# A hybrid encoder layer: the out-projection by Strassen's seven products

## The chip, the cores and the metric

One core of a Trainium2 chip runs the whole kernel. The metric is the device time of one execution in microseconds (us): the median of three runs, and for where the time goes one profiled execution. TensorE is PE in the profile, VectorE DVE, ScalarE ACT, GpSimd POOL, and SP is the engine whose queue issues the transfers.

## The reference

One layer of a hybrid encoder: the input is projected (`w_in`), half of the heads are gMLP heads, half a state space model (SSD); their outputs side by side go through the out-projection `w_out` (2048 to 1024). Then come a residual sum with LayerNorm, a feed-forward part with a squared relu, and a residual sum with LayerNorm again.

```python
def layer_norm(x, g, b):
    ...
    y = (xf - mu) * lax.rsqrt(var + LN_EPS) * g.astype(jnp.float32) + b.astype(jnp.float32)
    ...
    out = jnp.einsum('ble,ed->bld', jnp.concatenate([y_g, y_s], axis=-1), w_out)
...
def squared_relu_ffn(x, w1, w2):
    h = jnp.square(jax.nn.relu(jnp.einsum('bld,df->blf', x, w1)))
    return jnp.einsum('blf,fd->bld', h, w2)
```

There are 2048 prompt tokens and 8 x 16 tokens of running streams, so 17 tiles of 128 tokens (`NCH`); `KD` is 8, a width of 1024 in tiles of 128. The scale of the SSD half's normalisation (`ssd_norm_g`) is multiplied into the rows of `w_out` that it meets.

## The kernel before

Every product in full precision is made of three matmuls (`PASSES`) of two parts: `split` (lines 55 and 56) rounds an operand on ACT into a first part and takes the rest on DVE as a second.

**Mixer** (`mixer_heads`). The tokens go in three blocks of 6, 6 and 5 tiles. In each block 18 weight units (x, z, u, v) are multiplied in a fixed order, and between units `run` takes one task of a list: an SSD step of a tile (`ssd`) or a gMLP step (`gmlp`). Block 0 splits the weights and stores the two parts (`keep_parts`); blocks 1 and 2 load the parts (line 117), which have twice the bytes of the raw weights. gMLP writes its outputs to DRAM by features (`yg`, 128 features x 128 tokens), SSD by tokens (`ys`). The last block's five gMLP tasks are left over as the tail.

**Out-projection** (`out_proj`). All of `w_out` is split once into eight tiles in SBUF (`load_w`, eight `wout` tiles). Token tiles go by groups, the first two and the last two together, the others one by one: `load_yg` and `load_ys` load a tile (SSD's by four transfers and a transposition by DVE, `flip`, line 43) and split it (`mx`); 96 matmuls of 128x512 (line 683) make its row of outputs; then come the residual sum and LayerNorm on DVE with scale and bias (`layer_norm`), and the store. The tail's tasks run within the first group. Beside it, `during_out_proj` makes in each group a piece of what FFN1 needs: four sums of a group of `w_ff1` weights (`w1_piece`, lines 777 to 780, on DVE, stored as `w1s`) and, three times, the sums of the transposed LayerNorm outputs (`x_piece`, stored as `xv`).

**FFN** (`ffn`). FFN1 is by Strassen's seven products already: for each of three token blocks and 16 weight groups, seven products of 12 matmuls (line 858), whose operands are the sums above. `load_x` and `load_w1` load and split them.

Order: each engine takes its instructions in one fixed order, which a scheduler has made from the order of the code and its own costs. SP issues all transfers in one such order; by the semaphores of the built program each transfer waits for the one eight before it.

## Time and profile before

| | us |
|---|---|
| median of three runs | 2825.11 (2823.72 to 2827.59) |
| the profiled execution | 2822.72 |
| its span | 2821.0 |
| PE busy | 2753.9 |
| DVE, ACT, POOL busy | 1816.1, 1096.0, 395.1 |
| mean granted clock of PE | 0.991 |

The 40 slices of the page show where PE is less than fully busy: the 8s at slices 16 and 21 are the beginning and the end of the out-projection, the last is the kernel's end.

```text
PE   9999999999999998999989999999999999999998
DVE  6766667645585457665558667667775356644887
ACT  5445423323333333100115556556665323333343
```

A digit is the busy share of a slice of 70.5 us in tenths; 9 is 90% or more. In a row of the groups of instructions the numbers behind the count are busy time and the mean of one in ns, then the idle time of the engine just before them and what ended it.

### The profile page before, as it was taken

How to read it: one execution, taken by the hardware profiler on the slowest of the kernel's cores; microseconds unless marked ns; L12 is line 12 of the kernel's file. 1: busy time of each engine (PE TensorE's matmuls, PEld its weight loads, DVE VectorE, ACT ScalarE, POOL GpSimd, SP SyncE). 2: the span in 40 equal slices, each digit the busy share in tenths (PEclk: the TensorE clock that was granted, in tenths of full speed). 3: DMA queues.
4: the chain of work that ended last, by engine and by line, in shares of the span. 5: the costliest groups of instructions: out<-in, count | busy, mean ns of one | idle time of the engine just before them, and what ended most of it. 6: DMA issues, size and time to landing. Idle time of an engine off the chain costs nothing.

```text
span 2821.0 us, 42133 instructions
## 1 busy us (share of the span) xinstructions
PE 2753.9 (98%) x15814; PEld 2525.6 (90%) x15814; DVE 1816.1 (64%) x2836; ACT 1096.0 (39%) x2024; POOL 395.1 (14%) x547
## 2 busy tenths in 40 slices
PE   9999999999999998999989999999999999999998
PEld 8988899999999997887879999999999888888886
DVE  6766667645585457665558667667775356644887
ACT  5445423323333333100115556556665323333343
POOL 2214223323233312000100000000000000000022
PEclk9999999999999999999999999999999999999999
DMA  9897888766697768888579858667877468855764
GB/s 316 257 297 250 281 288 272 228 221 217 218 305 220 244 218 302 279 260 273 159 217 342 292 214 286 222 223 259 276 233 259 152 233 300 299 173 190 272 206 171
DMA packets 492316, 699.83 MB, mean 248 GB/s; under 512 B 74560, under 2 KB 379088, under 8 KB 485584
## 3 DMA queue, kind: packets, MB, share of 16 engines
q1 hardware_dynamic: 492112, 697.14, 74.8%
q8 instruction: 124, 2.03, 0.3%
q14 instruction: 80, 0.66, 0.1%
HBM read 474.04 MB, written 223.00 MB: 247 GB/s over the span
## 4 chain that ended last, share of the span: by engine, by line
PE 77%; DMA 12%; DVE 6%; issue 1%; ACT 1%; POOL 1%; SPq 1%; DVEq 0%; ACTq 0%; POOLq 0%
PE pf L858 22%; PE pf L1075 22%; PE psfl L231 13%; PE pstl L239 10%; PE po L683 4%; PE yd L446 2%; DMA w1p<-in_w_ff 2%; DMA w1s<-w1p 2%; PE pf L1040 2%; DMA v<-v 1%; DMA xv<-xtt 1%; PE st L483 1%; DMA v<-vo 1%; DMA e<-at 1%; PE yo L489 1%
## 5 line engine op out<-in xcount | busy, mean ns | idle before, releaser
L858 PE MATMUL pf<-xt,w 128*128 128x384 f32 (+1 forms) x4032 | 671.8, 329 | 14.6 <-ACT w L55 11.4
L858 PEld LDWEIGHTS pf<-xt,w 128*128 128x128 f32 x4032 | 669.2, 189 | 17.4 <-ACT w L55 12.3
L1075 PE MATMUL pf<-w,ht 128*128 128x512 f32 x2688 | 618.2, 389 | 0.0
L1075 PEld LDWEIGHTS pf<-w,ht 128*128 128x128 f32 x2688 | 504.6, 188 | 104.6
L231 PE MATMUL psfl<-xw,w 128*128 128x384 f32 (+1 forms) x2880 | 494.9, 330 | 0.0
L231 PEld LDWEIGHTS psfl<-xw,w 128*128 128x128 f32 x2880 | 475.5, 188 | 9.0 <-issue 8.6
L239 PE MATMUL pstl<-w,xw 128*128 128x256 f32 (+1 forms) x3264 | 411.0, 286 | 8.4 <-ACT w L55 6.5
L239 PEld LDWEIGHTS pstl<-w,xw 128*128 128x128 f32 x3264 | 396.4, 190 | 21.0 <-issue 11.8
L683 PE MATMUL po<-wout,mx 128*128 128x512 f32 x1632 | 379.5, 394 | 12.0 <-ACT mx L55 8.1
L683 PEld LDWEIGHTS po<-wout,mx 128*128 128x128 f32 x1632 | 309.2, 190 | 79.1 <-ACT mx L55 8.8
L56 DVE TENSOR_TENSOR ht<-hr,ht 128x1536 fp32r<-128x1536 f32 (+1 forms) x84 | 132.3, 1577 | 128.0 <-ACT ht L55 126.5
L76 POOL TENSOR_SCALAR frs<-fmv 128x1 f32<-128x1 f32 x17 | 8.9, 524 | 1291.6 <-DVE fmv L996 1291.0
L55 ACT CAST ht<-hr 128x1536 fp32r<-128x1536 f32 (+1 forms) x84 | 112.2, 1337 | 194.7 <-PE pf L1075 142.0
L56 DVE TENSOR_TENSOR w<-w1s,w 128x512 fp32r<-128x512 f32 x192 | 132.0, 691 | 41.0 <-ACT w L55 36.0
L55 ACT CAST w<-w1s 128x512 fp32r<-128x512 f32 x192 | 118.3, 619 | 64.1 <-PE pf L858 57.0
L308 DVE SCALAR_TENSOR_TENSOR acc<-raw,cw,acc 128x640 f32<-128x640 f32 (+1 forms) x108 | 111.4, 1031 | 14.1 <-ACT acc L302 12.7
L56 DVE TENSOR_TENSOR w<-w2r,w 128x512 fp32r<-128x512 f32 x144 | 93.8, 686 | 36.8 <-ACT w L55 36.6
L55 ACT CAST w<-w2r 128x512 fp32r<-128x512 f32 x144 | 83.3, 618 | 87.3 <-PE pf L1075 56.9
L438 ACT ACTIVATE e<-e,nacum 128x128 f32<-128x128 f32 x272 | 83.6, 389 | 66.8 <-POOL e L69 66.7
L55 ACT CAST w<-w1r 128x512 fp32r<-128x512 f32 x96 | 59.4, 618 | 98.6 <-PE pf L858 95.3
L247 ACT ACTIVATE gt<-gt 128x256 f32<-128x256 f32 (+1 forms) x116 | 52.3, 451 | 95.9 <-DVE gt L246 95.9
L849 ACT ACTIVATE hc<-hc 128x384 f32<-128x384 f32 (+3 forms) x144 | 87.1, 608 | 1.8
(214 smaller groups left out, 2875.4 us busy)
## 6 DMA issues: line engine op xcount, KB each, us to landing
w1s<-w1s SPq DMA_DIRECT2D x48, 1024.0 KB, 6.7
hr<-hv SPq DMA_DIRECT2D x56, 768.0 KB, 6.1
w2r<-in_w_ff SPq DMA_DIRECT2D x112, 256.0 KB, 5.6
w<-w_x SPq DMA_DIRECT2D x12, 2048.0 KB, 10.5
w1r<-in_w_ff SPq DMA_DIRECT2D x48, 512.0 KB, 6.7
hv<-hs SPq DMA_DIRECT2D x32, 768.0 KB, 5.2
ws<-in_w_in SPq DMA_DIRECT2D x34, 512.0 KB, 7.7
e<-at SPq DMA_DIRECT2D x34, 512.0 KB, 6.7
```

What stands on the lines that cost most here:

```text
L55: nc.scalar.copy(hi, src)
L56: nc.vector.tensor_sub(lo, src, hi.bitcast(F32))
L231: nc.tensor.matmul(ps[:, :n], w[:, a, k, f * P:(f + 1) * P], xw[:, b, k, o:o + n], start=(q, i, k) == KORDER[0], stop=(q, i, k) == KORDER[-1])
L239: nc.tensor.matmul(ps[:, :n], xw[:, a, k, j * P:(j + 1) * P], w[:, b, k, :n], start=(q, i, k) == KORDER[0], stop=(q, i, k) == KORDER[-1])
L308: nc.vector.scalar_tensor_tensor(aa, raw[:, k:k + npr], cw[:, ft, k:k + 1], aa, op0=ALU.mult, op1=ALU.add)
L438: nc.scalar.activation(e[:, h], e[:, h], AF.Exp, bias=s["nacum"][:, i:i + 1])
L446: nc.tensor.matmul(yd[:, h * HD:(h + 1) * HD], e[:, h], xdt[:, h * HD:(h + 1) * HD], start=True, stop=True)
L683: nc.tensor.matmul(acc[c][d], m[c][k // 4][:, a, k % 4], W[q][:, w, i, d * 512:(d + 1) * 512], start=k == 0 and (a, w) == (0, 0), stop=k = ...
L849: nc.scalar.activation(t, t, AF.Square)
L858: nc.tensor.matmul(o, W[i][:, u, k], X[i][:, v, k, :n], start=q + k == 0 and not more, stop=q == 2 and k == 3, skip_group_check=True)
L1040: nc.tensor.matmul(ps[d], h[:, u, k, f], w[d][:, v], start=k + f + q == 0, stop=(k, f, q) == (n - 1, 1, 2))
L1075: nc.tensor.matmul(acc[l], h[:, u, m, j * P:(j + 1) * P], w[m][:, v], start=kg + q + m == 0, stop=(kg, q, m) == (3, 2, 3))
```

## The change

**Out-projection.** Tiles are taken in eight pairs: (0,3), (1,4), (2,5), (6,9), (7,10), (8,11), (12,14), (13,15); tile 16 is alone (`ODD`). A pair's rows, the two halves of the 2048 inputs (here: each half holds four feature tiles of gMLP and four of SSD) and the two halves of the outputs make a 2 x 2 product of matrices, which seven products of 24 matmuls (128x512) give. `seq` is their order: product 1, then 2, of the first six pairs; 1 and then 2 of the last two pairs and the odd tile; 0 of the odd tile; then 6, 7 and 5 of all pairs; then 4 and 3 by turns, and 3 of the odd tile. "(6,2)" is product 6 of pair 2. Each product has its own weight operand of eight tiles (`wo`), of which two sets fit; it is made from raw parts (`wor`, four buffers), for 6 with two subtractions whose results are stored (`wot`) for 5 and 4. The results are summed up in tiles `y` in SBUF (`evict`), by ACT for product 1 and DVE else.

**Sums of the left operand** (`mix`) are made in the mixer as tasks: for each pair four sums of the gMLP half and four of the SSD half, which is loaded by `flipped` (four transfers and a half transposition each), stored as `mv` in DRAM and loaded by `load_mix`. The last two pairs' and the odd tile's are left to the tail with the five gMLP steps.

**LayerNorm** of the first residual is only normalised in `finish` (by ACT); scale and bias are applied by features in `tokens` (eight ACT operations of 128x128 for each tile), and by tokens on POOL in `x1_piece` for the second residual. **Sums of `w_ff1`** are made by POOL in FFN1's first block. **Weight units**: the parts are kept for every other unit, nine of 18; the other nine are loaded raw and split again in each block. The pool `w4` has nine buffers.

```diff
+THIRDS = [([0, 1, 2], [3, 4, 5]), ([6, 7, 8], [9, 10, 11]), ([12, 13], [14, 15])]
+ODD = 16
...
-        if b > 0:
+        if u in parts:
             nc.sync.dma_start(w[:, :, :, :n].bitcast(F32), parts[u])
             return w
         for q in range(2):
             load_w_half(w, u, q)
-        keep_parts(u, w)
+        if order.index(u) % 2 == 0:
+            keep_parts(u, w)
...
+    partner = {r: (k, l) for k, (l, r) in enumerate(p for t in THIRDS for p in zip(*t))}
+    def flipped(c, q):
+        s = half("fs").rearrange("p (a f) -> p a f", a=4)
+        for i in range(4):
+            nc.sync.dma_start(s[32 * i:32 * i + 32],
+                              ys_d[c][:, 256 * i + 128 * q:256 * i + 128 * q + 128].rearrange("(a j) f -> j a f", j=32))
+        t = half("ft").rearrange("p (k t) -> p k t", k=4)
+        flip(nc, t, s)
+        return t
+    def mix(b, j):
+        r = BLOCKS[b][0] + j
+        if r == ODD:
+            for q in range(2):
+                nc.sync.dma_start(mv[-1][:, 4, 4 * q:4 * q + 4], flipped(r, q))
+        if r not in partner:
+            return
+        p, l = partner[r]
+        for part in range(2):
+            tile4 = lambda name: half(name).rearrange("p (k t) -> p k t", k=4)
+            if part == 0:
+                a11, a12, a21, a22 = (tile4("ma") for i in range(4))
+                for t, c, q in ((a11, l, 0), (a12, l, 1), (a21, r, 0), (a22, r, 1)):
+                    nc.sync.dma_start(t, yg_d[c][:, 4 * q:4 * q + 4])
+            else:
+                a11, a12, a21, a22 = (flipped(c, q) for c in (l, r) for q in range(2))
+                nc.sync.dma_start(mv[p][:, 4, :4], a11)
+                nc.sync.dma_start(mv[p][:, 4, 4:], a12)
+                nc.sync.dma_start(mv[p][:, 5, 4:], a22)
+            to = lambda v: mv[p][:, v, 4 * part:4 * part + 4]
+            s1, s2, s3 = (tile4(f"ms{i}") for i in range(3))
+            nc.vector.tensor_add(s1, a21, a22)
+            nc.sync.dma_start(to(2), s1)
+            nc.vector.tensor_sub(s2, s1, a11)
+            nc.sync.dma_start(to(0), s2)
+            nc.vector.tensor_sub(s3, a11, a21)
+            nc.sync.dma_start(to(1), s3)
+            nc.vector.tensor_sub(s1, a12, s2)
+            nc.sync.dma_start(to(3), s1)
...
+        while k and tasks:
+            f, *a = tasks.pop(0)
+            f(*a)
+            k -= f is not mix or a[0] == len(BLOCKS) - 1
...
-            tasks += [(gmlp, b, j) for j in range(n)]
+            if b < len(BLOCKS) - 1:
+                tasks += [(gmlp, b, j) for j in range(n // 2)]
+                tasks += [(f, b, j) for j in range(n // 2, n) for f in (gmlp, mix)]
+            else:
+                tasks += [(gmlp, b, j) for j in range(n)] + [(mix, b, j) for j in range(2, n)]
             if b == len(BLOCKS) - 1:
                 break
         run(1)
-    run(len(tasks) - BLOCKS[-1][1])
+    run(len(tasks) - BLOCKS[-1][1] - 3)
...
+    yl = pool("yl", 1)
+    wr = pool("owr", 4)
+    mp = pool("mo", 3)
+    mr = pool("mr", 2)
+    wq = pool("wq", 16)
...
+    made = [dr.tile([2, P, 2, 512], F32, name=f"wot{k}") for k in range(4)]
+    b11, b12, b21, b22 = ((f, d) for f in range(2) for d in range(2))
+    PARTS = {1: (b11,), 2: (b21,), 3: (b22,), 6: (b11, b12, b22), 7: (b12, b22), 5: (1,), 4: (2, b21), 0: (b12,)}
+    def load_part(t, part, k):
+        if isinstance(part, int):
+            nc.sync.dma_start(t, made[k][part - 1])
+            return
+        f, d = part
+        nc.sync.dma_start(t, A["w_out"][4 * (k // 2) + 2 * f + k % 2][:, :, 512 * d:512 * d + 512])
+        if k >= 2:
+            for m in range(2):
+                i = 4 * f + 2 * (k % 2) + m
+                nc.scalar.activation(t[:, m], t[:, m], AF.Copy, scale=ng[:, i:i + 1])
+    def load_w(i):
+        out = []
+        for k in range(4):
+            s = None
+            for n, part in enumerate(PARTS[i]):
+                t = wr.tile([P, 2, 512], F32, name="wor", tag="wr")
+                load_part(t, part, k)
+                if n:
+                    nc.vector.tensor_sub(t, t, s)
+                if n and i == 6:
+                    nc.sync.dma_start(made[k][n - 1], t)
+                s = t
+            for m in range(2):
+                w = wq.tile([P, 2, 512], F32R, name="wo", tag="w")
+                split(w[:, 0], w[:, 1], s[:, m])
+                out.append(w)
+        return out
...
+    V = {6: 0, 7: 1, 5: 2, 3: 3}
+    def load_mix(i, p):
+        s = mr.tile([P, KD, P], F32, name="mxs", tag="mr")
+        if p < len(pairs) and i in V:
+            nc.sync.dma_start(s, mv[p][:, V[i]])
+        else:
+            c = ODD if p == len(pairs) else pairs[p][i == 4]
+            k = slice(0, 4) if i in (0, 1) else slice(4, 8)
+            nc.sync.dma_start(s[:, :4], yg_d[c][:, k])
+            nc.sync.dma_start(s[:, 4:], mv[p][:, 5 if i == 4 else 4, k])
+        t = mp.tile([P, 2, KD, P], F32R, name="mx", tag="mx")
+        split(t[:, 0], t[:, 1], s)
+        return t
...
+    def finish(c, *halves):
+        for d in halves:
+            stat(c, d)
+        mean = small.tile([P, 2], F32, name="lmv")
+        nc.vector.bn_aggr(mean, stats[c])
+        rs = small.tile([P, 1], F32, name="lrs")
+        rsqrt(rs, mean[:, 1:2], 1.0, EPS)
+        nm = small.tile([P, 1], F32, name="lnm")
+        nc.gpsimd.tensor_scalar(nm, mean[:, 0:1], rs, -1.0, op0=ALU.mult, op1=ALU.mult)
+        nc.scalar.activation(y[c], y[c], AF.Identity, bias=nm, scale=rs)
+        nc.sync.dma_start(n1_d[c], y[c])
...
+    seq = [(i, p) for ps in (range(n - 2), (n - 2, n - 1, n)) for i in (1, 2) for p in ps] + [(0, n)] + [(i, p) for i in (6, 7, 5) for p in range(n)]
+    seq += [(4, 0)] + [s for p in range(n - 1) for s in ((4, p + 1), (3, p))] + [(3, n - 1), (3, n)]
+    order = list(dict.fromkeys(i for i, p in seq))
+    first = load_mix(*seq[0])
+    W = {order[0]: load_w(order[0])}
+    ahead = {seq[0]: first}
     pss = [ps]
...
+    at = 0
+    for k, (i, p) in enumerate(seq):
+        if i not in W or k == 0:
+            if i not in W:
+                W[i] = load_w(i)
+        nx = order.index(i) + 1
+        if nx < len(order) and order[nx] not in W and (p == 0 or i == 0) and (i, p) != (2, 0):
+            W[order[nx]] = load_w(order[nx])
+        if k + 1 < len(seq):
+            ahead[seq[k + 1]] = load_mix(*seq[k + 1])
+        mx = ahead.pop((i, p))
+        at += 1
+        if p < n - 2 and (i == 1 or i == 2 and p < 3):
+            tail(1)
+        acc = pss[at % len(pss)].tile([P, 512], F32, name="po", tag="a")
+        for q, (u, v) in enumerate(PASSES):
+            for m in range(KD):
+                nc.tensor.matmul(acc, mx[:, u, m], W[i][m][:, v], start=q + m == 0, stop=(q, m) == (2, KD - 1))
+        if (i, p) == (2, 3):
             tail(NCH)
             right.close()
             rpool = lambda name, bufs, **k: pool(name, bufs, side="right", **k)
             pss.append(rpool("pso", 4, space=PSUM))
...
+            yr = rpool("yr", 1)
+            y.update({c: yr.tile([P, D], F32, name=f"y{c}") for c in [r for l, r in pairs] + [ODD]})
+        evict(i, p, acc)
+        if i == 3 and 1 <= p <= 3:
+            sums.x_piece(0, p - 1)
...
-        load_blocks(self.nc, s, self.x1_d[c])
+        load_blocks(self.nc, s, self.n1_d[c])
         t = self.sp.tile([P, KD, P], F32, name="xtt", tag="st")
         flip(self.nc, t, s)
+        for k in range(KD):
+            self.nc.scalar.activation(t[:, k], t[:, k], AF.Identity, bias=self.gb[:, 1, k:k + 1], scale=self.gb[:, 0, k:k + 1])
...
-        a11, a21, a12, a22 = (w[k][:, :, f] for k in range(2) for f in range(2))
-        nc.vector.tensor_add(a22, a21, a22)
-        nc.vector.tensor_sub(a21, a11, a21)
-        nc.vector.tensor_sub(a11, a22, a11)
-        nc.vector.tensor_sub(a12, a12, a11)
-        for k in range(2):
-            nc.sync.dma_start(self.w1[g][:, k], w[k].rearrange("p k f n -> p (k f n)"))
...
-    wp = pool("w4", 10)
+    wp = pool("w4", 9)
...
+        nc.gpsimd.tensor_mul(t, t, gb[:, 0])
+        nc.gpsimd.tensor_add(t, t, gb[:, 1])
+        nc.sync.dma_start(x1_d[c][:, h], t)
...
-        w = wr.tile([P, 4, P], F32, name="w1l", tag="wr")
-        nc.sync.dma_start(w, A["w_ff1"][g][:, :4, :P])
+        w = wr.tile([P, 4, 2, P], F32, name="w1l", tag="wr")
+        if b == 0:
+            nc.sync.dma_start(w.rearrange("p k f n -> p k (f n)"), A["w_ff1"][g][:, :4])
+        else:
+            nc.sync.dma_start(w[:, :, 0], A["w_ff1"][g][:, :4, :P])
         v = wr.tile([P, 4, 2, P], F32, name="w1r", tag="wr")
         nc.sync.dma_start(v.rearrange("p k f n -> p k (f n)"), A["w_ff1"][g][:, 4:])
         s = sump.tile([P, 2, 4, 2, P], F32, name="w1s", tag="ws")
-        nc.sync.dma_start(s.rearrange("p h k f n -> p h (k f n)"), sums.w1[g])
-        return {1: w, 2: v[:, :, 0], 4: v[:, :, 1], 6: s[:, 0, :, 0], 7: s[:, 0, :, 1], 3: s[:, 1, :, 0], 5: s[:, 1, :, 1]}
+        flat = s.rearrange("p h k f n -> p h (k f n)")
+        a11, a21, a12, a22 = (t[:, :, f] for t in (w, v) for f in range(2))
+        s2, s3, s4, s1 = (s[:, h, :, f] for h in range(2) for f in range(2))
+        if b == 0:
+            nc.gpsimd.tensor_add(s1, a21, a22)
+            nc.gpsimd.tensor_sub(s2, s1, a11)
+            nc.gpsimd.tensor_sub(s3, a11, a21)
+            nc.gpsimd.tensor_sub(s4, a12, s2)
+            nc.sync.dma_start(sums.w1[g], flat)
+        else:
+            nc.sync.dma_start(flat, sums.w1[g])
...
+        for j in ([k - 14] if k >= 14 else []):
+            x1_piece(j)
```

Three places in the order. First the transfers on SP just ahead of the operand of (1,7), the first product of the last pair. Before, at the same stage of the program (late tiles of the out-projection), SP has loads of whole tiles and stores of results:

```order
L648 DMA mxs<-yg_90 128x1024
L37 DMA mys<-ys_107 32x4x256 x4
L703 DMA xr<-in_x 128x1024
L711 DMA x_11_121<-x_13678 128x1024
L648 DMA mxs<-yg_91 128x1024
```

Now, with `mv_151` the sums of pair 7 and `fs` the buffers of `flipped`:

```order
L570 DMA fs<-ys_106 32x4x128 x4
L592 DMA mv_151<-ft 128x512
L747 DMA xr<-in_x 128x512
L570 DMA fs<-ys_108 32x4x128 x4
L593 DMA mv_151<-ft 128x512
L731 DMA mxs<-mv_151 128x512
```

The operand of a product is now loaded (L731) right behind the store of its last part (L593), which waits for a transposition of what four loads bring.

Second, ACT around product 0 of the odd tile. Before, ACT's rows in the out-projection's middle are casts of operands alone, `mx<-mxs` and `mx<-myt` by turns. Now, with L772 the copy of (0,odd)'s result, L700 the scalings of raw parts and `wo` the weight operand of product 6:

```order
L772 COPY y_12821<-po 128x512
L57 CAST mx<-mxs 128x1024
L700 ACTIVATE wor<-wor,ng 128x512 x8
L57 CAST wo<-wor 128x512 x2
L700 ACTIVATE wor<-wor,ng 128x512 x4
L57 CAST wo<-wor 128x512 x6
```

Twelve scalings and eight casts for the weights of (6,0), the next product, come behind that copy.

Third, SP at the passage to FFN1. Before, with L819 the loads of FFN1's left operands:

```order
L711 DMA x_13_123<-x_13968 128x1024
L37 DMA xts<-x_6_116 32x4x256 x4
L37 DMA xts<-x_9_119 32x4x256 x3
L819 DMA xr<-xv_11517 128x1536
L703 DMA xr<-in_x 128x1024
```

Now the same loads are L929, with L762 the last stores of the out-projection, `n_16` that of the odd tile, and L952 the store of the sums that POOL makes:

```order
L762 DMA n_13_123<-y_12069 128x1024
L762 DMA n_16_126<-y_12821 128x1024
L952 DMA w1s_12029<-w1s 128x2048
L880 DMA xv_12027<-xsum 128x4x128
L877 DMA xv_12027<-xtt 128x4x128
L881 DMA xv_12027<-xsum 128x4x128
L883 DMA xv_12027<-xtt 128x4x128
L885 DMA xv_12027<-xtt 128x4x128
L929 DMA xr<-xv_12026 128x1536 x2
```

The first loads of FFN1's left operands stood ahead of the last tiles' residual loads, and stand behind the last tile's store now.

More of the change, by code (lines that the diff above doesn't have):

```diff
@@ L601, in mixer_heads @@
     return run
[L604 to L613 removed]
+ORDER = (1, 6, 2, 7, 5, 4, 3)
@@ L616, in out_proj @@
+NG = 16
+TOKENS = (384, 384, 320)
+PAIRS = (384, 384, 256)
 @with_exitstack
-def out_proj(ctx, tc, right, ps, tail, A, dr, small, sp, rsqrt, split, yg_d, ys_d, x1_d, done):
+def out_proj(ctx, tc, right, ps, tail, A, dr, small, sp, rsqrt, split, yg_d, mv, n1_d, sums):
     nc = tc.nc
     pool = lambda name, bufs, **k: ctx.enter_context(tc.tile_pool(name=name, bufs=bufs, reuse_waits="tile", **k))
-    wps = [pool(f"wo{q}", 1) for q in range(8)]
-    mp = pool("mo", 6)
-    ring = pool("wp", 2)
+    yl = pool("yl", 1)
[3 more added lines that the diff above has]
+    wq = pool("wq", 16)
@@ L640, in split_mix @@
-    def split_mix(c, src):
-        for q in range(2):
-            t = mp.tile([P, 2, 4, P], F32R, name="mx", tag="mx")
-            split(t[:, 0], t[:, 1], src[:, 4 * q:4 * q + 4])
-            m.setdefault(c, []).append(t)
-    def load_yg(c):
-        s = sp.tile([P, KD, P], F32, name="mxs", tag="st")
-        nc.sync.dma_start(s, yg_d[c])
-        split_mix(c, s)
-    def load_ys(c):
-        s = sp.tile([P, 4, 256], F32, name="mys", tag="st")
-        load_blocks(nc, s, ys_d[c])
-        t = sp.tile([P, KD, P], F32, name="myt", tag="st")
-        flip(nc, t, s)
-        split_mix(c, t)
@@ L658, in out_proj @@
[L658 to L689 removed]
+    pairs = [p for t in THIRDS for p in zip(*t)]
@@ new lines, in out_proj @@
+    y = {l: yl.tile([P, D], F32, name=f"y{l}") for l, r in pairs}
+    made = [dr.tile([2, P, 2, 512], F32, name=f"wot{k}") for k in range(4)]
[11 more added lines that the diff above has]
+                nc.scalar.activation(t[:, m], t[:, m], AF.Copy, scale=ng[:, i:i + 1])
```

177 lines of the change are left out of this document (77 added, 100 removed).

## The prediction

> **What bounds the kernel now.** I read the page first, then the windows by stage, the waits of PE in the stages that lose time, PE's timeline there, and last the groups and transfers for durations. The page:
>
> ```profile
> PE 2753.9 (98%) x15814; PEld 2525.6 (90%) x15814; DVE 1816.1 (64%) x2836; ACT 1096.0 (39%) x2024; POOL 395.1 (14%) x547
> L683 PE MATMUL po<-wout,mx 128*128 128x512 f32 x1632 | 379.5, 394 | 12.0 <-ACT mx L55 8.1
> L636 ACT ACTIVATE wout<-wos,ng 128x1024 fp32r<-128x1024 f32 x8 | 9.2, 1152 | 23.5 <-DMA wos<-in_w_out 23.4
> ```
>
> PE is busy for 98% of the span, so removed matmuls count in full as long as PE is still fed. The windows (mixer's second and third block, then four stretches of the out-projection, then FFN1) show where it isn't:
>
> ```profile
> core 0: us, PE busy (x) PEld busy (x) DVE busy (x) ACT busy (x) POOL busy (x), PEclk, DMA share, GB/s
> 460.00:800.00 340.00, 338.44 (x2369) 326.39 (x2368) 201.40 (x353) 111.16 (x275) 101.91 (x125) 1.00 0.72 232
> 800.00:1050.00 250.00, 248.00 (x1790) 236.98 (x1789) 149.21 (x235) 83.91 (x221) 75.50 (x95) 0.99 0.75 243
> 1050.00:1130.00 80.00, 70.81 (x394) 60.19 (x393) 59.93 (x110) 24.58 (x36) 20.78 (x20) 0.96 0.86 289
> 1130.00:1330.00 200.00, 198.37 (x876) 163.91 (x874) 123.64 (x174) 21.48 (x36) 15.78 (x18) 1.00 0.87 271
> 1330.00:1430.00 100.00, 95.50 (x410) 78.84 (x411) 56.81 (x78) 13.28 (x22) 10.80 (x12) 0.97 0.50 154
> 1430.00:1500.00 70.00, 58.48 (x256) 50.54 (x255) 45.91 (x56) 18.30 (x23) 3.37 (x5) 0.88 0.94 296
> 1500.00:2152.00 652.00, 648.92 (x3933) 647.76 (x3932) 461.65 (x786) 385.38 (x678) 0.00 (x0) 1.00 0.74 256
> ```
>
> From 1050 to 1500 us PE idles for 9.2 + 1.6 + 4.5 + 11.5 = **26.8 us**. Those go with the old out-projection; what the new one idles is to be set against them. The mixer's two later blocks idle 3.6 us of 590, FFN1 3.1 us of 652: nothing to win there, only to lose. PE's timeline at the end of the out-projection and the clock in the same place:
>
> ```profile
> 1463.65 4.24 PE L683 MATMUL po<-wout,mx 128*128 128x512 f32 x18
> 1474.66 4.71 PE L858 MATMUL pf<-xt,w 128*128 128x384 f32 x12 [6.76 <-ACT w L55]
> 1483.99 17.69 PE L858 MATMUL pf<-xt,w 128*128 128x384 f32 x84 [4.62 <-ACT w L55]
> 1503.87 4.37 PE L858 MATMUL pf<-xt,w 128*128 128x384 f32 x15 [2.19 <-ACT hc L861]
> ```
>
> ```profile
> 1474.60:1479.40 4.80, 4.58 (x12) 3.56 (x12) 4.80 (x8) 1.48 (x2) 0.33 (x1) 0.50 1.11 358
> 1487.00:1490.00 3.00, 3.00 (x11) 3.00 (x11) 3.00 (x7) 2.06 (x3) 0.00 (x0) 0.50 1.09 317
> 1490.00:1494.00 4.00, 4.00 (x25) 4.00 (x23) 4.00 (x5) 2.19 (x4) 0.00 (x0) 0.99 1.06 308
> ```
>
> A stall costs more than its length. After the gap of 6.8 us the granted clock is 0.50, and 12 matmuls take 4.58 us; at 0.99, 25 take 4.00, so 12 would take 1.92. Each new stall of over some 5 us is priced at **2 us** on top, between 0 and these 2.7. In the Trainium skill, "TensorE: Matmul & The Clock Gate", part 1 says that the gate halves the clock after an idle window of about 3.4 us and needs as long a busy stretch to open; by it a stall would cost 1.7 us on top, close to the row.
>
> **What is removed.** Before, 17 tokens' tiles x 2 halves x 48 matmuls = 1632. After, 8 pairs x 7 products x 24 = 1344, and 4 x 24 = 96 for the odd tile: 1440. In the undisturbed window 198.37 us / 876 = 0.2265 us each, so 192 x 0.2265 = **-43.5 us**, and a product of 24 lasts 5.4 us. They all stand on PE, which is the path: no cover has to be asked for. Whether PE is fed decides.
>
> **What is added, on PE's way.** Durations:
>
> ```profile
> ys<-xs SPq DMA_DIRECT2D x34, 256.0 KB, 2.9
> mxs<-yg SPq DMA_DIRECT2D x17, 512.0 KB, 4.4
> wos<-in_w_out SPq DMA_DIRECT2D x16, 512.0 KB, 6.8
> xr<-xv SPq DMA_DIRECT2D x14, 768.0 KB, 7.3
> L55 ACT CAST w<-w1s 128x512 fp32r<-128x512 f32 x192 | 118.3, 619 | 64.1 <-PE pf L858 57.0 <-DMA w1s<-w1s 5.1 <-DVE w L56 1.9
> L56 DVE TENSOR_TENSOR w<-w1s,w 128x512 fp32r<-128x512 f32 x192 | 132.0, 691 | 41.0 <-ACT w L55 36.0
> L55 ACT CAST w<-ws 128x1024 fp32r<-128x1024 f32 x34 | 34.2, 1048 | 2.9 <-DMA ws<-in_w_in 2.7
> L56 DVE TENSOR_TENSOR w<-ws,w 128x1024 fp32r<-128x1024 f32 x34 | 42.5, 1271 | 5.7 <-ACT w L55 5.5 <-issue 0.2
> L55 ACT CAST xt<-xr 128x1536 fp32r<-128x1536 f32 x14 | 20.7, 1477 | 41.1 <-DMA xr<-xv 21.5 <-PE po L683 19.6
> L546 POOL TENSOR_TENSOR ug<-ug,og 128x512 f32<-128x512 f32 x34 | 56.6, 1674 | 46.4 <-DVE og L545 40.9 <-ACT raw L301 3.9 <-DMA wos<-in_w_out 1.5
> L441 POOL TENSOR_TENSOR xdt<-xs,dt 128x512 f32<-128x512 f32 x34 | 36.9, 1086 | 128.5 <-DMA xs<-xs 128.5
> L43 DVE STREAM_TRANSPOSE myt<-mys 128x1024 f32<-128x1024 f32 x17 | 21.1, 1244 | 18.3 <-DMA mys<-ys 18.2
> ```
>
> *Start.* W_out's first tiles used to be split between the gelus of the last v unit. In the new order ACT does nothing for the out-projection until v3's last gelu; W1's raw loads stand behind the last SSD store on SP. So: raw load 6.8, four scalings of 128x512 at 0.62 = 2.5 (two lie in the load of the next part), eight casts at 0.62 = 5.0, the operand's cast 1.05: 15.4 at most, less about 1 for loads that leave a little before v3's last matmul. I take **14**, between 9 (loads landed, 2.5 + 5.0 + 1.05) and 16.
>
> *The last pairs' operand sums.* The tail's three mixes cannot begin before the last gMLP heads, six products in, about 36 us after the first out-projection matmul. Product 1 of the last pair, tiles (13,15), is due after 6 + 6 + 1 = 13 products, at 70. Between lie, on SP in program order, about 75 transfers (a flip takes four), of which each waits for the one eight before it: 9.4 turns, and with the two places where a sum or a flip stands between (about 1.5 turns) I count 11. With 7 us of DVE and ACT work on the way (four half flips at 0.62, two sums at 0.69, a cast of 1.05, queues) the operand is there at 36 + 11 L + 7, L being one transfer's time: a stall of 11 L - 27. The odd tile's operand comes four turns and 3 us after it, and is due one product later: another 4 L - 2.4. With the 2.9 and 4.4 us of the rows the two stalls are 4.9 + 9.2 = 14 and 21.4 + 15.2 = 37 us. These DMAs are of 256 KB or less, in a stretch that lost the transfers of the W1 sums, so I take L = 3.1, near the lower row: 7.1 + 10 = **17**.
>
> *W6.* Product 6 needs twelve raw parts of W_out in four raw buffers. ACT takes the scalings of its second half only behind the copy of product 0's result. From there: 12 scalings and 8 casts at 0.62 = 12.4 us, one reload into a freed buffer 6.8, of which about half is hidden by scalings, and a last subtraction and cast of about 2. Of these 18 us a part goes on under the last matmuls; I take **14**, in 7 to 20. The changes to W7, W5, W4 and W3 have 8 products (43 us) each for 8 or fewer parts: **2**, in 0 to 5.
>
> *To FFN1.* W1's raw buffers lie where out-projection weights lay until the last matmul, so their loads start then, as before. But before, the first two X loads were issued by then; now they stand on SP behind the odd tile's store and behind the store of the sums that POOL makes of W1. So: raw load 6.8, five POOL ops at 1.09 to 1.67 = 5.4 to 8.4, X load 7.3, its cast 1.5, together 21 to 24, of which the store of the last tile hides nothing. I take **21**, in 12 (if the X loads aren't held up) to 24.
>
> That is 14 + 17 + 14 + 2 + 21 = 68 us of idle time for the 26.8 that go: **+41.2**. Three more stalls at half clock, less one in the transition, at 2 us: **+4**.
>
> **What is added beside PE.** In blocks 1 and 2 of the mixer DVE gets six pairs x (8 sums x 0.69 + 4 flips of 128x512 at half of 1.244) = 48 us, and for the nine units that are split again two subtractions of 1.27 each, 23 us per block; with 201.40 of 340 before, that is about 248 (73%). The matmuls hide it. SSD and gMLP steps share the buffers of half size with the mixes and can come late: 0 to 8. FFN1 block 0: POOL was at 0.00 and gets four 128x512 ops per weight group, 4.4 to 6.7 us. A group of block 0 has 84 matmuls:
>
> ```profile
> L858 PE MATMUL pf<-xt,w 128*128 128x384 f32 x2688 | 474.3, 339 | 14.2 <-ACT w L55 11.4 <-ACT hc L861 2.2 <-ACT xt L55 0.5
> L501 DVE TENSOR_TENSOR xs<-xs,yt 128x512 f32<-128x512 f32 x32 | 31.6, 988 | 0.7
> L56 DVE TENSOR_TENSOR mx<-mxs,mx 128x512 fp32r<-128x512 f32 x34 | 23.8, 711 | 12.3 <-ACT mx L55 12.3
> ```
>
> 84 x 474.3 / 2688 = 14.8 us, so the load (6.8 for 512 KB, above), the sums and a split (1.3) just fit when made one group ahead. The DVE add L501, which reads two SBUF tiles beside POOL's multiplications, takes 0.988 us where a like op takes 0.711, so splits beside POOL may stretch by 0.3 us; seven a group, 2 us, fit. LayerNorm's scale and bias go from two DVE passes to ACT, which has room (21.48 of 200 us), and to POOL behind FFN1. FFN's w4 pool has nine buffers rather than ten. For all of this I take **+7**, in 0 to 20: the reserves are there, but in every one of these stages PE idles under 1.5% already, so that any disorder counts.
>
> The Trainium skill, "GPSIMD Engine Reference", section 8, says that POOL shares its SBUF interfaces with VectorE, with contention for DVE instructions that read two SBUF inputs: it speaks against W1's sums on POOL; L501's row agrees, and by the rule the seven splits and the four sums of a group would both stretch.
>
> **Sum.** -43.5 + 41.2 + 4 + 7 = +8.7. Against the profiled execution's 2822.7 us that is 2831.4; it lies 2.4 below the median of the runs shown (2825.1), so I say **2834 us**, slower by 0.3%. About 0.2%, 5.7 us, is what a measurement of this kernel can tell from no change.
>
> **Rivals.** *(a) The saving stands (faster).* Place: the three new stalls. The turns take 2.9 us or less, since a 256 KB store takes 2.9 even in the mixer's full DMA; the scalings are spread under products (2,7) and (0,odd); the X loads overtake. Then 9 + 14 + 7 + 0 + 14 = 44 us of idle time, +17, no more half clock, +1 beside PE: -43.5 + 17 + 1 = -25, **2800 us**. For it speaks that the page's ACT is idle 61% of the span; against it, that all three stalls follow from the order in which one engine issues, which no idle share mends. It decides against mine when the sum of idle time in the out-projection stays below 60 us. *(b) POOL's sums hold up FFN1 (slower by much).* Place: the 16 weight groups of block 0. With raw load 6.8 + four sums at 1.67 = 6.7 + split 1.3 = 14.8 us in series, the group's own 14.8 us has no reserve; if the raw buffers (three, for two loads a group) make the loads wait for the sums of the group before, each group is about 1.5 us late: +24, **2858 us**. For it: L546's 1.674 on the same shape, beside DVE work; against it: L441's 1.086 where DVE is not in the way, and the sums may run a group ahead. It decides from 1.5 us per sum upward. That the change does not do what it says cannot be: the count of matmuls is fixed, and each has the old one's shape.
>
> **How the numbers follow.** Mine 0.48, with a range of its own from 2820 to 2848; (a) 0.32, of which a tenth lies above 2819; (b) 0.20. Faster by over 0.2% (below 2819.5): 0.32. That is (a) but for 0.03, and 0.03 of mine. Within (to 2830.8): 0.17 of mine and 0.03 of (a), 0.20. Slower: the other 0.28 of mine and (b), 0.48. The range, leaving out a third of (a) and a third of (b): 2800 to 2862.
>
> **What would show it.** In the changed profile: PE idle 8 to 16 us ahead of the first po, a gap ahead of product (1,7) and another ahead of (1,odd), both ended by ACT's cast mx, a gap behind (0,odd) ended by wo, and one of over 15 us ahead of the first pf that an X load or its cast ends. Windows of FFN1's block 0 with PE under 97% would show (b). It is wrong if the out-projection idles less than 50 us in all, or if the mixer's blocks lose more than 15.

## The result, and the profile after

The changed kernel takes **2940.23 us** (median of four runs, 2933.95 to 2943.47), against 2826.35 for the kernel before in the same comparison: a ratio of **1.040**, 95% interval 1.0375 to 1.0418. I had said 2834, slower by 0.3%, in 2800 to 2862: the sign was right, the size far off. The profiled execution took 2943.47 us, its span is 2941.5.

The page of the changed kernel, in the form of the rows shown of before:

```profile
span 2941.5 us, 42988 instructions
PE 2745.7 (93%) x15622; PEld 2509.6 (85%) x15622; DVE 1993.3 (68%) x2969; ACT 1266.1 (43%) x2303; POOL 607.7 (21%) x696
PE   8999999999999998769956998999999999999998
L981 PE MATMUL pf<-xt,w 128*128 128x384 f32 (+1 forms) x4032 | 682.3, 331 | 77.2 <-ACT xt L57 56.8
L831 PE MATMUL po<-wo,mx 128*128 128x512 f32 x1440 | 343.0, 400 | 58.6 <-ACT mx L57 37.7
```

PE is busy 8.2 us less, and idles 195.8 us where it had idled 67.1. The matmuls are gone as forecast: 343.0 us of po for 379.5. But a po matmul costs 0.238 us for 0.2325, and FFN1's cost 10.5 us more in all: with more stalls the mean granted clock fell from 0.991 to 0.969. The waits of PE in the changed kernel, by what ended them (total, times, longest):

```profile
PE pf L981 <- ACT xt L57: 56.8, 5, 39.2
PE po L831 <- ACT mx L57: 37.7, 7, 13.5
PE po L831 <- ACT wo L57: 21.0, 3, 12.3
PE pf L981 <- DVE hc L992: 15.3, 7, 4.2
PE sg L546 <- DVE v L535: 8.6, 5, 3.5
PE yd L455 <- POOL xdt L450: 8.1, 7, 1.9
```

The stalls of the prediction ahead of the first po, (1,7) and (1,odd) are in the second row and product 6's in the third; the longest wait of the first row is the passage to FFN1. What isn't in the prediction at all is small in each wait and large in sum. The table takes each stage from its first matmul to its last in the traces, or to the first of the next block where blocks follow one another (a mixer block by its z and v matmuls, `pstl`: 6, 6 and 5 of 17 parts of the 3264; an FFN1 block has 1344).

| stage, us | before | after | difference |
|---|---|---|---|
| mixer, block 0 | 382.2 | 388.8 | +6.6 |
| mixer, block 1 | 365.6 | 386.2 | +20.6 |
| mixer, block 2 | 311.2 | 325.9 | +14.7 |
| to the first po | 2.9 | 13.5 | +10.6 |
| out-projection | 399.6 | 394.9 | -4.7 |
| to the first FFN1 matmul | 6.8 | 39.2 | +32.4 |
| FFN1, block 0 | 247.4 | 276.6 | +29.2 |
| FFN1, block 1 | 233.7 | 243.8 | +10.1 |
| FFN1, block 2 | 203.7 | 204.9 | +1.2 |
| FFN2 | 647.6 | 647.6 | 0.0 |

These add up to 120.7 us, for 120.5 between the two spans. **82 us lie in stages that have no matmul of the change in them** (mixer and FFN1); the stages with the change's matmuls and the two passages beside them cost 38. The same stretch of both mixers by the windows view, first before, then after:

```profile
core 0: us, PE busy (x) PEld busy (x) DVE busy (x) ACT busy (x) POOL busy (x), PEclk, DMA share, GB/s
400.00:1050.00 650.00, 643.18 (x4522) 619.23 (x4521) 385.21 (x672) 213.94 (x542) 196.27 (x241) 0.99 0.74 240
```

```profile
400.00:1050.00 650.00, 621.97 (x4284) 598.87 (x4283) 422.90 (x726) 221.97 (x523) 177.85 (x210) 0.98 0.78 245
```

After, PE gets 238 matmuls less done in the 650 us. At before's mean of 0.142 us of busy time for one (643.18 / 4522), that is 34 us: it idles 21 us more, and the other 13 are matmuls that take longer on average, 0.145 us. Much of that goes with the granted clock: it falls to 0.50 for 3 to 7 us behind six of some fifteen gaps of 0.5 to 3.5 us. No engine is near its end: DVE is at 65%.

PE's timeline at the stalls that were forecast, first product (1,7), then (1,odd), then the weights of product 6; the last two rows are the end of the out-projection and the first FFN1 matmuls:

```profile
1216.03 8.11 PE L831 MATMUL po<-wo,mx 128*128 128x512 f32 x24 [13.46 <-ACT mx L57]
1231.84 29.79 PE L831 MATMUL po<-wo,mx 128*128 128x512 f32 x124 [7.70 <-ACT mx L57]
1264.42 1.31 PE L831 MATMUL po<-wo,mx 128*128 128x512 f32 x4 [2.80 <-ACT wo L57]
1280.79 2.92 PE L831 MATMUL po<-wo,mx 128*128 128x512 f32 x6 [12.35 <-ACT wo L57]
1289.53 14.05 PE L831 MATMUL po<-wo,mx 128*128 128x512 f32 x54 [5.81 <-ACT wo L57]
1504.89 11.17 PE L831 MATMUL po<-wo,mx 128*128 128x512 f32 x48 [1.26 <-ACT mx L57]
1555.30 6.41 PE L981 MATMUL pf<-xt,w 128*128 128x384 f32 x24 [39.24 <-ACT xt L57]
```

### The profile page after: what moved, and what is told of

It is laid out like the page before. It is cut to its first block, busy times and chain, and to the rows that moved or that the text cites. A ratio compares the mean times of both kernels' runs of the same rounds, so it can differ in the third digit from the quotient of the medians.

```text
span 2941.5 us, 42988 instructions
## 1 busy us (share of the span) xinstructions
PE 2745.7 (93%) x15622; PEld 2509.6 (85%) x15622; DVE 1993.3 (68%) x2969; ACT 1266.1 (43%) x2303; POOL 607.7 (21%) x696
## 4 chain that ended last, share of the span: by engine, by line
PE 58%; DMA 19%; DVE 10%; issue 4%; ACT 3%; POOL 3%; SPq 3%; DVEq 0%; POOLq 0%; ACTq 0%
PE pf L1200 21%; PE pf L981 15%; PE pstl L248 7%; PE po L831 5%; PE psfl L240 5%; DMA e<-at 2%; DVE w L58 2%; PE yd L455 2%; PE pf L1165 1%; DMA fs<-ys 1%; DMA ma<-yg 1%; DVE acc L317 1%; DMA yg<-ug 1%; DMA xts<-n 1%; DMA wor<-in_w_out 1%
## 5 line engine op out<-in xcount | busy, mean ns | idle before, releaser
L981 PE MATMUL pf<-xt,w 128*128 128x384 f32 (+1 forms) x4032 | 682.3, 331 | 77.2 <-ACT xt L57 56.8
L248 PEld LDWEIGHTS pstl<-w,xw 128*128 128x128 f32 x3264 | 399.6, 191 | 23.0 <-issue 7.8
L831 PE MATMUL po<-wo,mx 128*128 128x512 f32 x1440 | 343.0, 400 | 58.6 <-ACT mx L57 37.7
L831 PEld LDWEIGHTS po<-wo,mx 128*128 128x128 f32 x1440 | 276.6, 193 | 121.2 <-ACT mx L57 40.5
L58 DVE TENSOR_TENSOR w<-w1s,w 128x512 fp32r<-128x512 f32 x192 | 160.0, 835 | 31.5 <-ACT w L57 27.5
L57 ACT CAST mx<-mxs 128x1024 fp32r<-128x1024 f32 x60 | 62.6, 1047 | 130.7 <-DMA mxs<-mv 62.0
L58 DVE TENSOR_TENSOR w<-ws,w 128x1024 fp32r<-128x1024 f32 (+1 forms) x72 | 91.5, 1289 | 8.8 <-ACT w L57 8.7
L58 DVE TENSOR_TENSOR w<-w1r,w 128x512 fp32r<-128x512 f32 x96 | 82.7, 862 | 19.8 <-ACT w L57 19.5
```

Source lines behind the costliest of these rows:

```text
L57: nc.scalar.copy(hi, src)
L58: nc.vector.tensor_sub(lo, src, hi.bitcast(F32))
L248: nc.tensor.matmul(ps[:, :n], xw[:, a, k, j * P:(j + 1) * P], w[:, b, k, :n], start=(q, i, k) == KORDER[0], stop=(q, i, k) == KORDER[-1])
L831: nc.tensor.matmul(acc, mx[:, u, m], W[i][m][:, v], start=q + m == 0, stop=(q, m) == (2, KD - 1))
L981: nc.tensor.matmul(o, W[i][:, u, k], X[i][:, v, k, :n], start=q + k == 0 and not more, stop=q == 2 and k == 3, skip_group_check=True)
```

## The experiments

Each edit is on the changed kernel unless it says before. "Blocks 1 and 2" are the mixer's, taken as in the table: 676.8 us before, 712.1 after. What they differ by from trace to trace is seen in runs whose edit lies outside the mixer: 704.0 to 714.3 us with the mixes, and in the three kernels without any mix 674.0, 676.5 and 682.1. Differences below 10 us are no evidence here.

### Which part of the change slows the mixer

**All parts kept.**

```diff
-        if order.index(u) % 2 == 0:
-            keep_parts(u, w)
+        keep_parts(u, w)
```

> The changed kernel, but with the parts of all 18 weight units kept, as before. The mixer became 43 us longer with the change. Theory M (the mixes: DVE's sums and flips wait in its order for SP's transfers, and the convolution and gating behind them come late): the mixer gets back at most 12 us, 2928 to 2942 us in all. Rival S (the second splitting of nine units in blocks 1 and 2, 23 us of DVE and of ACT a block, makes the units late): 30 us or more come back, 2895 to 2912 us.

Measured: 2945.55 us; blocks 1 and 2 take 718.0. Nothing comes back.

**No mixes.** The tasks are left out of the list, and `load_mix` loads from the gMLP outputs:

```diff
-            nc.sync.dma_start(s, mv[p][:, V[i]])
+            nc.sync.dma_start(s, yg_d[c])
```

> The changed kernel without any mix: the operand sums are left out, and every product's operand is loaded from the gMLP outputs, in transfers of the same sizes. Theory M: the mixer gets back 30 us or more, and the stalls ahead of (1,7) and (1,odd), 13.5 + 7.7 us, go too: 2875 to 2895 us. Rival S: the mixer keeps 30 of its 43 us, and only the two stalls go: 2910 to 2930 us.

Measured: 2870.33 us, 70 less. Blocks 1 and 2 take 674.0, the out-projection 361.1 instead of 394.9. The mixes cost 38 us in these blocks and 34 in the out-projection: in sum more than the 43.5 us that the products were to save.

**Half of the parts, alone, in the kernel before.** The same condition as in the changed kernel's `load_w`.

> The kernel before, with the parts kept for every other unit alone. Theory M: within 10 us of before, 2820 to 2836 us. Rival S: 25 us or more slower than before, 2850 to 2870 us. Both, if it is the sum of DVE's work that counts: 2835 to 2850 us.

Measured: 2834.9 us, ratio 1.0017 (1.0003 to 1.0031), blocks 1 and 2 at 677.5. The weight parts are not it.

**The mixes alone, in the kernel before.** `flipped`, `mix` and the tasks as in the diff of the change; nothing reads `mv`.

> The kernel before, with the mixes alone added as tasks in the same places as in the changed kernel (their results are stored and not read). Theory M: the mixer takes 25 us or more longer, and the tail's mixes a few more in the out-projection: 2855 to 2880 us. Rival S: under 15 us, 2826 to 2840 us.

Measured: 2906.85 us, ratio 1.0277: blocks 1 and 2 take 714.5 (+37.7), and the out-projection 440.4 (+40.8), where the tail's mixes stand in DVE's order ahead of the residual sum that frees PE's accumulators. A PE wait of this run:

```profile
PE po L729 <- DVE xr L754: 31.9, 1, 31.9
```

So the mixes are the cause in the mixer, whichever kernel they stand in.

### What of the mixes does it

My theory was DVE's order. In the changed kernel DVE waits in the mixer for what the mixes load and store (420 to 1100 us: total, times, longest):

```profile
DVE ft L45 <- DMA fs<-ys: 31.5, 15, 4.7
DVE ms L597 <- DMA ma<-yg: 14.8, 4, 5.4
DVE ms L603 <- DMA mv<-ms: 9.6, 6, 2.5
```

**Transfers only.** `flipped` returns what it loaded, and the loaded tiles are stored without sums:

```diff
-            s1, s2, s3 = (tile4(f"ms{i}") for i in range(3))
-            nc.vector.tensor_add(s1, a21, a22)
-            nc.sync.dma_start(to(2), s1)
...
+            for v, t in ((2, a21), (0, a11), (1, a22), (3, a12)):
+                nc.sync.dma_start(to(v), t)
```

> The changed kernel with mixes that only move data: DVE's flips and sums are left out, each transfer of a mix is kept in its place (what is loaded is stored again). Without any mix the mixer's blocks 1 and 2 had lost 38 of their 35 us. Theory D (DVE waits in its own order for the mixes' transfers, and what stands behind it is late): nearly all comes back, blocks 1 and 2 within 8 us of the 365.6 and 311.2 us of before, and the out-projection 10 to 20 us shorter: 2885 to 2905 us. Rival R (SP's queue and the ring of eight half-size buffers, which the mixes' transfers fill): blocks 1 and 2 keep 25 us or more: 2915 to 2940 us.

(The second sentence of this text means: without any mix the two blocks became 38 us shorter; they had lost 35.) Measured: 2943.97 us, blocks 1 and 2 at 716.6. DVE is free of the mixes, and nothing is won in sum (block 1 is 11 us shorter, block 2 15 longer): **the theory fell**. Those 56 us of DVE's waits looked like a cause, and were none.

**From DRAM to DRAM.** The same number and sizes of transfers, without buffers in SBUF and without DVE:

```diff
-                    nc.sync.dma_start(t, yg_d[c][:, 4 * q:4 * q + 4])
+                    nc.sync.dma_start(scr[p][16 + k].rearrange("p (k t) -> p k t", k=4), yg_d[c][:, 4 * q:4 * q + 4])
```

> The changed kernel with mixes that take neither DVE nor a buffer in SBUF: all flips and sums are left out, and each of a mix's transfers, in the same number and sizes, goes from DRAM to DRAM. With transfers through the ring and without DVE's part the mixer had kept its loss. Theory G (the ring of eight half-size buffers, which gMLP and SSD share with the mixes: these come late, because their buffers do): blocks 1 and 2 come back to within 8 us of 365.6 and 311.2 us. Rival Q (SP's queue: its order, eight transfers in flight, issue time): they keep 25 us or more of their 35.

Measured: 2920.64 us, blocks 1 and 2 at 704.2: 27 of the 35 us stay, and the 8 that went are no more than traces differ by.

**Ten half-size buffers.**

```diff
-    fp = pool("fp", 8, right, side="right")
+    fp = pool("fp", 10, right, side="right")
```

> The changed kernel with ten half-size buffers instead of eight. Theory G: blocks 1 and 2 become 10 us or more shorter, together under 702 us (712.1 in the changed kernel, 676.8 before). Rival Q: within 6 us of 712.

Measured: 2932.63 us, blocks 1 and 2 at 708.0, 4 less: no share of the ring is shown.

**Stores of the mixes on POOL's queue.**

```diff
-            nc.sync.dma_start(to(2), s1)
+            nc.gpsimd.dma_start(to(2), s1)
```

> The changed kernel with the mixes' stores issued by POOL's queue, so that SP no longer waits in its order for a sum or a flip that it has to store (43 of the 59 us that SP waits at a mix's transfers). Rival Q in the form that SP's order counts: blocks 1 and 2 become 10 us or more shorter than 712. Theory G: within 6 us of 712, since the buffers are held as long.

Measured: 2926.77 us, blocks 1 and 2 at 708.3. SP's waiting for what it has to store does not make the loss either.

**Many small transfers, few large ones.** Both from DRAM to DRAM. The first copies 8 partitions of 128 in each of 31 transfers a pair, the second whole tiles:

```diff
-                nc.sync.dma_start(to(v), yg_d[c][:, 4 * q:4 * q + 4])
+                nc.sync.dma_start(mv[p][:8, v, 4 * part:4 * part + 4], yg_d[c][:8, 4 * q:4 * q + 4])
```

```diff
+            for k, c in enumerate((l, r)):
+                nc.sync.dma_start(scr[p][part, k], ys_d[c] if part else yg_d[c].rearrange("p k t -> p (k t)"))
+            for k, c in enumerate((l, r, l)[:2 + part]):
+                nc.sync.dma_start(mv[p][:, 3 * part + k], yg_d[c])
```

> As the kernel whose mixes copy from DRAM to DRAM, with the same number of transfers, but a sixteenth of the bytes in each; the mixes' arithmetic is left out, and the out-projection's operands are the gMLP outputs. That kernel's blocks 1 and 2 took 704.2 us together, 674.0 without any mix. Theory C (the number of transfers: SP issues them one by one, in order, with eight in flight): 692 us or more. Rival W (their bytes: the critical loads take longer beside them): 684 us or less.

> The same, with nearly the bytes of the full mixes (4.5 of 4.8 MB a pair), but in 9 transfers of 512 KB instead of 31; the arithmetic left out in the same way. Theory C: blocks 1 and 2 together 684 us or less. Rival W: 692 us or more.

Measured: 2914.35 us with blocks 1 and 2 at **705.3** for the many small ones, 2892.9 us and **683.8** for the few large ones. The windows of the two, in this order:

```profile
400.00:1050.00 650.00, 626.01 (x4284) 600.76 (x4283) 406.65 (x676) 233.62 (x552) 209.27 (x238) 0.98 0.66 208
```

```profile
400.00:1050.00 650.00, 638.91 (x4457) 613.84 (x4457) 415.75 (x702) 239.32 (x569) 212.65 (x242) 0.99 0.78 253
```

The same stretch without any mix, and with the 31 full-size transfers from DRAM to DRAM:

```profile
400.00:1050.00 650.00, 643.98 (x4542) 621.23 (x4541) 427.76 (x713) 242.13 (x576) 212.50 (x241) 1.00 0.66 211
```

```profile
400.00:1050.00 650.00, 626.58 (x4291) 600.02 (x4290) 410.91 (x688) 235.01 (x556) 213.59 (x242) 0.98 0.80 251
```

With many small transfers the DMA share is 0.66, as without mixes, and PE does 4284 matmuls, as few as in the changed kernel. With nearly all the bytes in 9 transfers the share is 0.78, and PE does 4457. It is **the number of transfers**: 31 a pair cost 30 us (full size) and 31 us (a sixteenth of it) against the 674.0 us without mixes. What 9 a pair cost is not told from nothing: their 683.8 us lie 10 above that kernel, and 2 above another one without mixes. By the issues of the changed kernel's trace 500 transfers start in these 650 us, 318 before.

Each of these programs also gets an order of its own for the other instructions. PE takes its work in the mixer in the same order, but for two places in some 320 stretches of like matmuls, in the runs with 31 and with 9 transfers of nearly the same bytes; so their 20 us do not come from PE's order (DVE's and ACT's agree to 95 and 97%). The run of the small ones has another order (90 to 93% of the stretches agree), and so has the changed kernel (83% with the kernel without mixes): that bytes count for little rests on runs with different orders, and what the order adds to the changed kernel's own loss was not tried.

What of a transfer counts, its issue on SP or that each waits for the one eight before it, was not tried apart. It is not that SP stands waiting at the mixes' own transfers: in the stretch above that takes 14 us in sum in the run with 31 full-size transfers, and 12 us in that with 9. Nor are longer landings the cause, as far as the medians show: gMLP's loads of v and u land in 5.4 and 5.5 us with the 31, and in 6.0 and 6.0 with the 9. From before to after, some landings became longer (SSD's stores `ys`, 2.1 to 4.3 us) and some shorter; the two rows are the loads of gMLP's v in this stretch, before and after:

```profile
v<-v SPq DMA_DIRECT2D x23, 256.0 KB, 6.1
```

```profile
v<-v SPq DMA_DIRECT2D x23, 256.0 KB, 5.0
```

### FFN1 and the passage to it

**Sums of W1 on DVE.**

```diff
-            nc.gpsimd.tensor_add(s1, a21, a22)
+            nc.vector.tensor_add(s1, a21, a22)
...
```

> The changed kernel with FFN1's sums of W1 on DVE instead of POOL. Block 0 of FFN1 takes 276.6 us against 247.4 before, and the splits beside POOL take 1.05 us against 0.69. Theory P (contention of POOL's two-input ops with DVE's): 4 x 0.69 = 2.8 us a group for some 7 x 0.36 + 4 x 0.45 = 4.3 us of stretching, block 0 becomes 10 to 25 us shorter: 2915 to 2930 us. Rival B (the sums stand between the raw load and the split, and three raw buffers let nothing run ahead): block 0 within 6 us of 276.6, 2934 to 2946 us.

Measured: 2924.99 us, FFN1's block 0 at 255.8 instead of 276.6 (blocks 1 and 2 are 5 and 4 longer than in the changed kernel). The groups of DVE in that block: the changed kernel, this run, and the kernel before.

```profile
L58 DVE TENSOR_TENSOR w<-w1s,w 128x512 fp32r<-128x512 f32 x64 | 67.1, 1050 | 8.0 <-ACT w L57 7.6
```

```profile
L58 DVE TENSOR_TENSOR w<-w1s,w 128x512 fp32r<-128x512 f32 x66 | 52.9, 805 | 2.1 <-ACT w L57 2.0
```

```profile
L56 DVE TENSOR_TENSOR w<-w1s,w 128x512 fp32r<-128x512 f32 x68 | 46.7, 690 | 15.8 <-ACT w L55 13.6
```

Beside POOL's work the same split takes 1.05 us, half as long again; it still takes 0.81 where only the work on the second residual is left on POOL (below), and 0.69 as before in the last run, which has nothing on POOL in this block:

```profile
L58 DVE TENSOR_TENSOR w<-w1s,w 128x512 fp32r<-128x512 f32 x59 | 40.2, 686 | 6.4 <-ACT w L57 6.0
```

In the changed kernel DVE is busy for 223.3 of the 252 us from 1580 to 1832, where the kernel before has 155.5 of 222. Behind the first 25 us of the block PE waits for DVE and ACT to empty an accumulator (`hc`, the fourth row of the waits), and never for a weight `w`, as it would if the sums in series with the loads made the weights late. (In the first 25 us it waits some 12 us, most of it for X operands, with the sums on either engine, and 7 in the kernel before.) Doing the sums on the engine that is short costs less than doing them beside it.

**Scale and bias of the second residual left out.**

```diff
-        nc.gpsimd.tensor_mul(t, t, gb[:, 0])
-        nc.gpsimd.tensor_add(t, t, gb[:, 1])
```

> The changed kernel, the scale and bias of the second residual left out (POOL's two ops in each of 34 pieces; the pieces are still loaded and stored). Theory P: block 1 of FFN1 (243.8 against 233.7 us before), where POOL has nothing else to do, comes back to within 3 us, and block 0 becomes up to 4 us shorter (2 of the 34 pieces): 2924 to 2934 us. Rival: block 1's loss is transfers or buffers, less than 4 us comes back: 2936 to 2945 us.

Measured: 2922.37 us (2916.28 to 2928.46). Block 1 takes 241.5, so only 2.3 of its 10 us come back, and block 0 266.4, ten less. I had taken two of the pieces to fall into block 0; POOL's group in that block of the changed kernel shows 17:

```profile
L912 POOL TENSOR_TENSOR x1t<-x1t,gb 128x512 f32<-128x512 f32 x17 | 27.3, 1612 | 34.4 <-DMA x1t<-n 28.5 <-DVE hc L986 5.8
```

**Buffers for the residual.**

```diff
-        x = sp.tile([P, 512], F32, name="xr", tag="st")
+        x = rx[0].tile([P, 512], F32, name="xr", tag="rx")
```

> The changed kernel with four buffers of their own for the residual's loads of x, which shared the small ring with FFN1's operand sums. Theory Q (in the out-projection's last products the x loads wait for that ring, LayerNorm of the last six tiles piles up behind them, and the stores, the weight buffers of FFN1 and the X loads behind these come late): the passage to FFN1 falls from 39.2 us to 10 to 22, 2908 to 2926 us. Rival (the X loads wait for POOL's sums and their store): 33 us or more stay, 2930 to 2942 us.

Measured: 2927.01 us, just outside the 2926; the passage takes 23.5 instead of 39.2. SP's rows in the changed kernel: the last stores of LayerNorm, POOL's sums' store, the first X loads.

```profile
1511.58 6.39 SPq L747 DMA_DIRECT2D xr<-in_x  x6
1535.18 3.12 SPq L762 DMA_DIRECT2D n<-y  x4
1539.04 0.32 SPq L952 DMA_DIRECT2D w1s<-w1s  x1
1548.31 0.99 SPq L929 DMA_DIRECT2D xr<-xv  x2
```

And in this run:

```profile
1519.08 1.15 SPq L931 DMA_DIRECT2D xr<-xv  x2
1532.15 0.75 SPq L954 DMA_DIRECT2D w1s<-w1s  x1
```

In the changed kernel six residual loads go out in one burst 4 us before the last matmul ends; everything behind them on SP comes after it. With buffers of their own the X loads go out at 1519, 9 us behind the last matmul instead of 32, and no longer stand behind the store of the sums. Of the 16 us won in the passage, 6 are lost again in FFN1's block 0 (282.8); blocks 1 and 2 of the mixer, which the edit leaves alone, are 8 shorter in this trace.

**Nine w4 buffers, alone, in the kernel before.**

```diff
-    wp = pool("w4", 10)
+    wp = pool("w4", 9)
```

> The kernel before with nine buffers in the FFN's pool w4 instead of ten, alone. In the changed kernel block 1 of FFN1 takes 243.8 us against 233.7, of which leaving out POOL's scale and bias gave back 2.3. If the tenth buffer is the reason: block 1 takes 240 to 244 us and block 2 and FFN2 also lose, 2835 to 2850 us. Rival (the pieces' transfers and POOL's claim on SBUF): within 2 us of 233.7, 2826 to 2833 us.

Measured: 2832.0 us, ratio 1.0004 (0.9984 to 1.0025), block 1 of FFN1 at 233.5. Not the reason.

**Six raw buffers in the out-projection.**

```diff
-    wr = pool("owr", 4)
+    wr = pool("owr", 6)
```

> The changed kernel with six raw buffers for the weights of the out-projection instead of four. PE waits 20.9 us in three gaps for product 6's weights. If the buffers are the reason: 10 us or more come back in the out-projection (394.9 us), 380 to 386. Rival (ACT's scalings stand behind the copy of product 0's result, whatever the buffers): under 5 us, 390 to 396.

Measured: the out-projection takes 385.6 us, 9.3 less, and PE waits 8.6 us for `wo` instead of 21.0. The buffers made more than half of it. The time of the whole, 2934.32 (2925.79 to 2942.85), is not clear of 2940.

### Taken together

**No mixes, W1's sums on DVE, buffers for the residual**: the edits of three runs above in one.

> The changed kernel without any mix (left out as in the second run), with FFN1's sums of W1 on DVE and with four buffers of their own for the residual's loads. If the three losses lie in different stages and add up: 2870 - 15 - 13 = 2842 us, still over the kernel before even with mixes that cost nothing. Rival (the stages feed one another, so that one gain is lost in the next): 2855 to 2872 us.

Measured: 2837.78 us, ratio 1.0025 (1.0008 to 1.0042): within 5 us of the sum, they add up.

**The same without scale and bias by features.**

```diff
-            x1_piece(j)
+            pass
...
-        for k in range(KD):
-            self.nc.scalar.activation(t[:, k], t[:, k], AF.Identity, bias=self.gb[:, 1, k:k + 1], scale=self.gb[:, 0, k:k + 1])
```

> The kernel of the run before without LayerNorm's scale and bias by features: the eight ACT operations of each token tile and the 34 pieces for the second residual, with their transfers, are left out too. If these make block 1 of FFN1 longer (243.8 us against 233.7, of which POOL's arithmetic was 2.3): block 1 falls to 233 to 236 us, and the whole to 2815 to 2830 us. Rival (w1l's larger tiles or the order of x pieces): block 1 stays over 240 us, 2832 to 2842 us.

Measured: 2817.52 us, ratio 0.9953 (0.9925 to 0.998); block 1 of FFN1 at 235.3, block 0 at 249.8. So the features' work with its pieces makes block 1's 10 us, and some more in block 0. Much of block 1's is one wait of PE for the cast of an X operand: 5.4 us in the changed kernel, 8.0 in the run before this one, 2.0 here. Only here, with mixes and LayerNorm's scale left out, is the kernel faster than before, and by 14 us (2831.28 in the same comparison) rather than 43: 8 of the rest are at the start (11.2 for 2.9), 16 in the passage (22.9 for 6.8), and PE still waits 17.1 us for product 6's weights. None of the changed kernel's variants that compute everything comes near the kernel before; the nearest takes 2925 us.

## Why the prediction was wrong

Its own signs spoke against it: the mixer's blocks were to lose no more than 15 us and lost 42, and PE, at 93.6% from 1580 to 1832 us, is below the 97% that was to show rival (b). Point by point, by its own steps:

- **The matmuls.** Right: 192 fewer, the po group falls by 36.5 us (43.5 were said). The other 7 go with the granted clock, 0.93 in the out-projection for 0.98 before.
- **The start.** Right: 14 us said, 12.6 measured between the last sg and the first po.
- **The last pairs' sums.** Right in place and nearly in size: 7.1 + 10 said, 13.5 + 7.7 measured. The size was in part luck: the count of turns gave anything from 14 to 37 us by the time taken for a turn, and no run measured the turns. That the transfers of the other pairs would count in the mixer, I did not see.
- **Product 6's weights.** Right in place, 14 said and 21.0 measured. ACT's scalings behind a copy, to which most of it was put down, are at most the smaller part; six raw buffers instead of four take 12.4 of it away.
- **To FFN1.** 21 said, 39.2 measured. I placed the X loads behind the store of the sums, and that is where they were, but took the last tiles' LayerNorm to be done in time. It wasn't: the residual's x loads share a ring with the x pieces, and went out in a burst at the end; with buffers of their own the passage takes 23.5. The step counted what is issued, and not when buffers come free for it.
- **"The matmuls hide it"**, the step on the mixer, 0 to 8 us: this failed, as the mixer lost 42, the largest miss beside FFN1. I counted DVE's work (48 + 46 us), found room for it, and left SP out, with a DMA share of 0.72 before me. DVE's work was indeed hidden (without it nothing is won). But 186 added transfers in two blocks were not. The runs show the number of transfers as the cause, at an estimated 0.17 us each (31 us for 186); by which way it acts stays open.
- **POOL's sums.** I took 0.3 us of stretch for each of seven splits and called it a fit; it was 0.36 for the splits, and DVE's other ops with two SBUF inputs were stretched too (the sums `hs`, from 0.55 us to between 0.94 and 1.16). Rival (b) named the stage and the sums, and 24 us; block 0 lost 29, of which 21 go with the sums. Its mechanism, sums in series with loads and splits, is not what the runs show; the contention is. The Trainium skill's "GPSIMD Engine Reference", section 8, which names this contention without a size, spoke against the edit; the trace agrees, with 1050 ns against 690.
- **LayerNorm by features.** Costed at next to nothing, within the 7 us for all that lay beside PE, with POOL's part behind FFN1; 17 of its 34 pieces lie in block 0. It costs 10 us in block 1 and some 11 in block 0 (249.8 against 261.1).
- **Half clock.** 2 us for each new long stall was fair: the granted clock is 0.50 for 4.3 us behind the stall ahead of the first po, and for 5.1 behind that of (1,7). That some fifteen gaps of 0.5 to 3.5 us in the mixer go with some 13 us beyond the 21 that they add was not in it.

In one sentence: the paths that I walked through were found in the right places but cost 38 us net where 2 were said (-43.5 + 41.2 + 4), and the 7 us set down for all that lay "beside PE" stood for 82.

## What to carry to other kernels

Where PE is at 98%, every stage that gets new work is priced on its own, transfers included: count a change's transfers per stage, and try what they cost alone, since here some two hundred small ones cost PE time without any engine or any bandwidth being full. A saving of matmuls by Strassen's scheme has to pay for its operand sums; here these cost 70 us for 43. And what an engine waits for is a clue, not a cause: DVE's 56 us of waiting for the mixes' loads vanished in a run, and the time did not.
